# Attention kernel of four blocks: order of gate products in the second half, and the Newton steps of 1/sqrt

## The chip, the cores and the metric

One core of a Trainium2 chip runs the whole program. The metric is the device time of one execution in microseconds; the time shown is the median of three runs. TensorE (PE) multiplies matrices, VectorE (DVE) and ScalarE (ACT) work on tiles in SBUF and on PE's results in PSUM, GpSimd (POOL) does some additions and memsets, and SyncE (SP) issues most of the DMAs.

## What is computed

A sequence of 512 tokens of width 1024 goes through one block with a neighbourhood and a dilated attention between two feed-forward parts, and then through two hybrid layers. The change touches the hybrid layers and every norm. One hybrid layer, cut to what matters:

```python
h = rmsnorm(x, mix_norm)                     # x * rsqrt(mean(x*x) + eps) * gain
z = h @ w_in                                 # queries, keys, values of three attentions, latents
o_a = nsa_attention(...)                     # 8 heads: compressed keys + selected + window
o_b = swa_sink_attention(...)                # 8 heads, band of 128 keys
o_c = mla_attention(...)                     # 8 heads from two normed latents
g = sigmoid(h @ w_branch_gate)               # 512 x 3072
g_a, g_b, g_c = split(g, 3)
merged = g_a * (o_a @ w_branch_a) + g_b * (o_b @ w_branch_b) + g_c * (o_c @ w_branch_c)
x = x + merged @ w_out
```

The compressed keys and values of `nsa_attention` come from a small network, `gelu(flat @ w1) @ w2`, on overlapping blocks of 32 tokens (`compress_blocks`).

## The kernel before

Every fp32 product is split: weights and activations are each a high part and a low part (`whi`, `wlo`, `uh`, `ul`), and `gemm` (lines 143 to 145) multiplies three pairs of them for each of 8 blocks of 128 rows, so one product of 128 columns of weights with 512 tokens is 24 matmuls of 128x512. ACT makes the high part (line 88), DVE the low part (line 89).

`mix2` works on one hybrid layer. The banded attention `swa` runs 8 heads in 8 steps, then `nsa` runs 8 heads, then `mla` 8 heads. Their own matmuls are small and wait for ACT and DVE in turn: scores on PE, maximum on DVE, exponential on ACT, scaling to two fp16 parts on ACT and DVE (`halves`, lines 98 and 99), transposes on PE (line 105 in the banded attention, 995 in the others), copies on ACT, product with the values on PE (lines 1002 and 1003). Between the heads `mix2` calls `pump`, which lets generators emit other work: projections of queries and keys (`qb`, `qa`, `kva`), the compression network (`inp`, `cmp_`, `end`), the latents of `mla` (`lt`), and `gts`, the gates. One step of `gts` is one gate product: 24 matmuls, a multiplication on DVE (line 470), a tanh on ACT (line 471) and a DMA to DRAM. There are 24 such steps in a layer. Two steps share one weight load of 1 MB into `wraw`, of which there are two buffers. `gt` is the gates' tile, with two buffers. The compression network also takes its two work tiles, `hT` and `s`, from `gt`.

```python
plan = ((qb, 1, kva, 1), (inp, 1, qb, 1), (inp, 1, cmp_, 1), (qb, 1, cmp_, 1), (qa, 1, cmp_, 1), (qa, 1, cmp_, 1),
        (qa, 1, end, 1, gts, 1), (kva, 1, qa, 1, gts, 1))
for n, _ in enumerate(self.swa(QB, *kb, i, OB)):
    self.pump(*plan[n])
plan = ((lt, 2), (lt, 2, gts, 1), (lt, 1, gts, 2)) + ((gts, 3),) * 5
for h, _ in enumerate(self.nsa(QA, KS, KW, KC, VS, VC, G, OA)):
    self.pump(*plan[h])
```

So two gates stand beside `swa` (after steps 6 and 7), 18 beside `nsa`, and the last four beside the first heads of `mla` (two after each head). What is emitted is not yet the order: a scheduler of the framework (a simulated timeline) orders the instructions of each engine when the program is built, and may bring independent work forward. On the chip each engine then keeps to that order.

`rstd` (lines 165 to 188) is 1/sqrt for all norms. PE adds up squares with a column of ones (line 171), DVE forms the mean (line 173), a first guess from the bits of the number (line 175), and three steps of three instructions each on 128x2 or 128x4 numbers (lines 177 to 179). Then DVE multiplies a diagonal with the result (line 185) and PE spreads it over all partitions as a row (line 186). It is called 21 times.

Of the kernel before, what the change touches and what calls it, by code (L numbers as in the profile page):

```python
# [13 lines left out]
OP = mybir.AluOpType  # L14
# [12 lines left out]
class Core:  # L27
# [135 lines left out]
    def rstd(self, acc, n, row=True, cols=ALL, stat=None):  # L163

        nc = self.nc
        st, r = stat or self.stat(row)
        js = range(cols.start // 128, cols.stop // 128)
        s = slice(js.start, js.stop)
        ps = self.bank(self.aside)
        for j in js:  # L170
            nc.tensor.matmul(ps[:, j:j + 1], acc[:, j * 128:(j + 1) * 128], self.ones[:, 0:1], start=True, stop=True)
        a, y, t = st[:, 0, s], st[:, 1, s], st[:, 2, s]
        nc.vector.tensor_scalar(a, ps[:, s], 1.0 / n, EPS, op0=OP.mult, op1=OP.add)

        nc.vector.tensor_scalar(y.bitcast(I32), a.bitcast(I32), -0.5, 1597463007.0, op0=OP.mult, op1=OP.add)
        for _ in range(3):
            nc.vector.tensor_tensor(t, y, y, op=OP.mult)
            nc.vector.scalar_tensor_tensor(t, t, -0.5, a, op0=OP.mult, op1=OP.mult)
            nc.vector.scalar_tensor_tensor(y, t, 1.5, y, op0=OP.add, op1=OP.mult)
        if r is None:  # L180
            return st[:, 1], r
        ps = self.bank(self.aside)
        for j in js:
            d = self.dtile("dr")
            nc.vector.tensor_scalar(d, self.ident, st[:, 1, j:j + 1], None, op0=OP.mult)
            self.row_done = nc.tensor.matmul(ps[:, j * 128:(j + 1) * 128], self.ones, d, start=True, stop=True).ins
        nc.scalar.activation(r[:, cols], ps[:, cols], AF.Copy)
        return st[:, 1], r
# [5 lines left out]
    def gain(self, x, g):  # L194
# [3 lines left out]
        return h, l  # L198

    def ffn(self, uh, ul, rstd, wg, wu, wd, sink, tail=None, first=None):  # L200


# [3 lines left out]
        def up(f0, nf):  # L206
            hh, hl = [], []
            for f in range(f0, f0 + nf, 2):
# [9 lines left out]
                for i in range(2):  # L218
                    if f == 0 and tail:
                        psg = banks[i]  # L220
                    else:
                        psg = self.bank()
                        self.gemm(psg, pg[i], uh, ul)
                    if f == 0 and tail and i == 0:
                        psu = banks[2]
                    else:
                        psu = self.bank()
                        self.gemm(psu, next(pu), uh, ul)
                    g = self.t("ft")
                    nc.vector.tensor_tensor(g, psg, rstd, op=OP.mult)  # L230
                    nc.scalar.activation(g, g, AF.Silu)
                    u = self.t("ft")
                    nc.vector.tensor_tensor(u, psu, rstd, op=OP.mult)
                    nc.vector.tensor_tensor(u, u, g, op=OP.mult)
                    h, l = self.t("hh", F32R), self.t("hl", F32R)
                    self.split(h, l, u)
                    hh.append(h)
                    hl.append(l)
# [606 lines left out]
class Block2(Block1):  # L845
# [205 lines left out]
    def mix2(self, X, U, a, i):  # L1051
        nc = self.nc
# [49 lines left out]
        def queries(out, first):  # L1102
            for c0 in (first, first + 256):
                for ps in proj(c0, 256):
                    out.extend(self.stack_q(self.rope(ps, cosr, sinr), 0.125))
                    yield

        def keys_a():
            for c0 in (768, 1024):
                ka.append(self.stack_k(self.rope(next(proj(c0)), cosr, sinr)))  # L1110
                yield

        def keys_b():
            kb.append(self.stack_k(self.rope(next(proj(1816)), cosr, sinr)))
            yield
            kb.append(self.values_b(next(proj(1944)), R))
            yield

        def gates():
            nonlocal gd  # L1120
            for gd in self.gates(a["w_branch_gate_2"][i], uh, ul, R, 24, f"gates2_{i}"):
                yield

        def branches():
            yield from self.branch(gd[8:16], a["w_branch_b_2"][i], OB, ("uh", "uh"), merged, "ul")
            yield from self.branch(gd[0:8], a["w_branch_a_2"][i], OA, ("uh", "uh"), merged, "ul")


        kvb, kva, qb, qa = keys_b(), keys_a(), queries(QB, 1304), queries(QA, 0)
# [3 lines left out]
        inp, cmp_ = self.compress_in(FL, i, proj, cosr, sinr, R, flat), self.compress(a, i, flat)  # L1133
        gts, brs, lt = gates(), branches(), self.latents(a, i, proj, w_in, uh, ul, R, lat)
        KC = VC = None

        def last():
            nonlocal KC, VC
            KC, VC = next(cmp_)
            yield  # L1140
        end = last()
        plan = ((qb, 1, kva, 1), (inp, 1, qb, 1), (inp, 1, cmp_, 1), (qb, 1, cmp_, 1), (qa, 1, cmp_, 1), (qa, 1, cmp_, 1),
                (qa, 1, end, 1, gts, 1), (kva, 1, qa, 1, gts, 1))
        for n, _ in enumerate(self.swa(QB, *kb, i, OB)):
            self.pump(*plan[n])
        KS, KW = ka


        plan = ((lt, 2), (lt, 2, gts, 1), (lt, 1, gts, 2)) + ((gts, 3),) * 5
        for h, _ in enumerate(self.nsa(QA, KS, KW, KC, VS, VC, G, OA)):  # L1150
            self.pump(*plan[h])
        for h, _ in enumerate(self.mla(lat, a, i, OC)):
# [69 lines left out]
    def compress(self, a, i, flat):  # L1222

        nc = self.nc
        out = []
        for kv in range(2):
            w1 = a["a_cmp_w1_v_2" if kv else "a_cmp_w1_k_2"][i]
            hT, s = self.t("gt"), self.t("gt")
            w2 = a["a_cmp_w2_v_2" if kv else "a_cmp_w2_k_2"][i].rearrange("(k p) n -> p k n", p=128)
            w = hT[:, 128:384].rearrange("p (k n) -> p k n", k=2)  # L1230
            nc.sync.dma_start(w[:, :, 0:64], w2)
            if kv == 0:
                nc.sync.dma_start(w[:, :, 64:128], w2)

            ps = self.bank()
            for half in range(2):
                r = self.raw(8, 256)
                nc.sync.dma_start(r, w1[1024 * half:1024 * half + 1024].rearrange("(k p) n -> p k n", p=128))
                for j in range(8):
                    e = j % 2  # L1240
                    nc.tensor.matmul(ps[64 * e:64 * e + 64, 0:256], flat[kv][:, 8 * half + j].rearrange("p g n -> p (g n)"),
                                     r[:, j], start=half == 0 and j < 2, stop=half == 1 and j > 5)
            nc.scalar.activation(s[0:64, 0:256], ps[64:128, 0:256], AF.Copy)
            nc.vector.tensor_tensor(s[0:64, 0:256], ps[0:64, 0:256], s[0:64, 0:256], op=OP.add)
            yield
            ps = self.bank()
            for m in range(2):
                nc.tensor.transpose(ps[:, 64 * m:64 * m + 64], s[0:64, 128 * m:128 * m + 128], self.ident[0:64, 0:64])
            nc.scalar.activation(hT[:, 0:128], ps[:, 0:128], AF.Gelu_apprx_tanh)
            yield  # L1250
            if kv == 0:
                both = self.t("kc", F32R)
                ps = self.bank()
                for k in range(2):
                    nc.tensor.matmul(ps[:, 0:64], w[:, k], hT[:, 64 * k:64 * k + 64], start=k == 0, stop=k == 1)
                c = both[:, 0:128].rearrange("p (g e n) -> p e g n", g=2, e=2)
                self.split(c[:, 0], c[:, 1], ps[:, 0:64].rearrange("p (g n) -> p g n", g=2))
                out.append([c[:, :, g] for g in range(2)])
            else:
                c = both[:, 128:384]  # L1260
                for g in range(2):
                    ps = self.bank()
                    for k in range(2):
                        nc.tensor.matmul(ps[0:32, 0:64], hT[:, 64 * k + 32 * g:64 * k + 32 * g + 32], w[:, k, 0:64],
                                         start=k == 0, stop=k == 1)
                    o = 128 * g
                    for r in (0, 32):
                        self.split(c[r:r + 32, o:o + 64], c[r:r + 32, o + 64:o + 128], ps[0:32, 0:64], 1 / UP)
                out.append([c[0:64, 0:128], c[0:64, 128:256]])
        yield out  # L1270
# [334 lines left out]
```

## Time and profile before

| | us |
|---|---|
| median of three runs | 3258.23 (3254.02 to 3265.27) |
| the profiled execution, its own time | 3259.47 |
| its span, first to last instruction | 3257.7 |
| PE busy | 3171.5 |
| DVE busy | 1905.7 |
| ACT busy | 1480.2 |
| POOL busy | 350.7 |
| mean granted clock of PE | 0.985 |

The granted clock is a share of 2.4 GHz: 1.00 in a stretch is that level throughout, 0.50 the lower level of 1.2 GHz. Matmuls overlap in PE, so that a busy PE is not always one at its peak. Of PE's busy time and of the chain that ended last, the page gives shares; of stretches of the span, a view by windows gives the busy time of each engine and the granted clock; the view of waits says which engine stood still, for how long in all, how often, and the longest of them.

The first hybrid layer's banded attention lies from about 1265 to 1385 us, its `nsa` from there to about 1620 us; in the second layer these are 2270 to 2385 us and up to 2621 us.

### The profile page before, as it was taken

Reading aid. Unit: us, or ns where it says so; the run is one execution under the profiler, and the core shown is the slowest. Engines: PE = TensorE matmul, PEld = TensorE weight load, DVE = VectorE, ACT = ScalarE, POOL = GpSimd, SP = SyncE. Lnnn points to the kernel's source line nnn. Section 1 sums busy time; section 2 is a strip of 40 time slices with the busy share of each in tenths; the row PEclk is TensorE's granted clock in tenths of the full one; section 3 lists DMA queues with packets and bytes.
Section 4 is the critical chain, followed back from the end, with each engine's and each line's share of the span. In section 5 each row is a group of like instructions: output and inputs, shape, how many; then the busy total and the mean of one; then the engine's idle time right before and its main releaser. Section 6 shows DMA issues by size and latency. Waiting matters only on the chain.

```text
span 3257.7 us, 44744 instructions
## 1 busy us (share of the span) xinstructions
PE 3171.5 (97%) x16695; PEld 2610.2 (80%) x16695; DVE 1905.7 (58%) x3745; ACT 1480.2 (45%) x2929; POOL 350.7 (11%) x562
## 2 busy tenths in 40 slices
PE   8999899999999998999999999999999999999998
PEld 7888888778888887778777888888778878788887
DVE  5344555555744458776677544357876677544355
ACT  4323335644432335667775322234766776322233
POOL 2200231102650020000003000000000002000001
PEclk9999999999999998999999999999989999999999
DMA  5432253336132325423265323224532246332322
GB/s 147 127 104 94 88 172 114 88 118 202 57 120 91 107 70 147 137 79 102 84 188 173 113 92 104 91 91 136 156 90 95 89 141 200 126 104 91 104 84 71
DMA packets 365737, 373.39 MB, mean 115 GB/s; under 512 B 48640, under 2 KB 317824, under 8 KB 365520
## 3 DMA queue, kind: packets, MB, share of 16 engines
q1 hardware_dynamic: 358672, 358.48, 35.5%
q0 software_dynamic: 6640, 12.01, 1.4%
q8 instruction: 131, 2.15, 0.3%
q14 instruction: 86, 0.70, 0.1%
q10 hardware_dynamic: 208, 0.05, 0.0%
HBM read 320.16 MB, written 44.91 MB: 112 GB/s over the span
## 4 chain that ended last, share of the span: by engine, by line
PE 91%; DVE 4%; DMA 2%; ACT 2%; issue 1%; SPq 0%; POOL 0%; DVEq 0%; ACTq 0%; POOLq 0%
PE ps_mm L143 13%; PE ps_mm L144 13%; PE ps_mm L145 13%; PE ps_s L145 6%; PE ps_s L143 6%; PE ps_s L144 6%; PE ps_t L143 6%; PE ps_t L145 6%; PE ps_t L144 6%; PE ps_s L969 3%; PE ps_t L995 2%; PE ps_o L1002 1%; PE ps_o L1003 1%; PE ps_t L105 1%; DMA gt<-gates 1%
## 5 line engine op out<-in xcount | busy, mean ns | idle before, releaser
L88 ACT ACTIVATE whi<-wraw 128x1024 fp32r<-128x1024 f32 (+4 forms) x422 | 414.7, 990 | 823.5 <-PE ps_mm L144 259.7
L143 PE MATMUL ps_mm<-uh,whi 128*128 128x512 f32 (+2 forms) x1648 | 647.0, 393 | 5.0 <-DVE ft L1041 2.8
L145 PE MATMUL ps_mm<-uh,wlo 128*128 128x512 f32 (+2 forms) x1648 | 644.2, 391 | 0.0
L144 PE MATMUL ps_mm<-ul,whi 128*128 128x512 f32 (+2 forms) x1520 | 593.6, 391 | 3.1 <-DVE ul L92 3.1
L89 DVE TENSOR_TENSOR wlo<-wraw,whi 128x1024 fp32r<-128x1024 f32 (+4 forms) x422 | 494.6, 1177 | 161.6 <-ACT whi L88 160.0
L143 PEld LDWEIGHTS ps_mm<-uh,whi 128*128 128x128 f32 (+1 forms) x1648 | 311.7, 189 | 65.9 <-DVE ft L1041 3.2
L145 PEld LDWEIGHTS ps_mm<-uh,wlo 128*128 128x128 f32 (+1 forms) x1648 | 311.0, 189 | 60.4 <-issue 0.2
L144 PEld LDWEIGHTS ps_mm<-ul,whi 128*128 128x128 f32 (+1 forms) x1520 | 287.2, 189 | 57.8 <-DVE ul L92 3.8
L143 PE MATMUL ps_t<-uh,whi 128*128 128x512 f32 (+1 forms) x600 | 231.2, 385 | 0.0
L145 PE MATMUL ps_t<-uh,wlo 128*128 128x512 f32 (+1 forms) x600 | 230.2, 384 | 0.0
L144 PE MATMUL ps_t<-ul,whi 128*128 128x512 f32 (+1 forms) x600 | 230.1, 383 | 0.0
L145 PE MATMUL ps_s<-uh,wlo 128*128 128x512 f32 (+1 forms) x544 | 208.6, 384 | 0.0
L144 PE MATMUL ps_s<-ul,whi 128*128 128x512 f32 (+1 forms) x544 | 208.6, 383 | 0.0
L143 PE MATMUL ps_s<-uh,whi 128*128 128x512 f32 (+1 forms) x544 | 208.4, 383 | 0.0
L88 ACT ACTIVATE dh<-wraw 128x768 fp32r<-128x768 f32 (+2 forms) x102 | 89.9, 898 | 209.1 <-PE ps_mm L144 68.8
L99 DVE SCALAR_TENSOR_TENSOR ph<-p,sa,ph 128x128 f16<-128x128 f32 (+2 forms) x224 | 124.6, 565 | 30.4 <-ACT ph L98 28.4
L89 DVE TENSOR_TENSOR dl<-wraw,dh 128x768 fp32r<-128x768 f32 (+2 forms) x102 | 105.1, 1044 | 62.6 <-ACT dh L88 62.2
L969 PE MATMUL ps_s<-k,q 128*128 128x256 f32 (+1 forms) x448 | 130.7, 383 | 2.4 <-ACT p L974 2.4
L144 PEld LDWEIGHTS ps_t<-ul,whi 128*128 128x128 f32 x600 | 114.8, 191 | 21.3
L143 PEld LDWEIGHTS ps_t<-uh,whi 128*128 128x128 f32 x600 | 114.7, 191 | 21.4
L145 PEld LDWEIGHTS ps_t<-uh,wlo 128*128 128x128 f32 x600 | 114.5, 191 | 21.6
L98 ACT ACTIVATE ph<-p,sa 128x128 f16<-128x128 f32 (+2 forms) x224 | 120.4, 554 | 25.0 <-DVE sa L990 18.7
(655 smaller groups left out, 6417.4 us busy)
## 6 DMA issues: line engine op xcount, KB each, us to landing
wraw<-w_in_in SPq DMA_DIRECT2D x28, 1024.0 KB, 5.4
wraw<-w_branch_gate_in SPq DMA_DIRECT2D x24, 1024.0 KB, 5.7
wraw<-ffn_w_gate_in SPq DMA_DIRECT2D x22, 1024.0 KB, 5.5
wraw<-ffn_w_up_in SPq DMA_DIRECT2D x22, 1024.0 KB, 5.4
wraw<-w_ffn_gate_in SPq DMA_DIRECT2D x22, 1024.0 KB, 5.9
wraw<-w_ffn_up_in SPq DMA_DIRECT2D x22, 1024.0 KB, 5.4
wraw<-ffn_w_down_in SPq DMA_DIRECT2D x24, 768.0 KB, 4.4
gates<-gt SPq DMA_DIRECT2D x64, 256.0 KB, 2.1
```

The costliest lines, as they stand in the source:

```text
L88: nc.scalar.activation(hi, src, AF.Copy)
L89: nc.vector.tensor_tensor(lo, src, hi.bitcast(F32), op=OP.subtract)
L98: self.nc.scalar.activation(h, P, AF.Copy, scale=scale)
L99: self.nc.vector.scalar_tensor_tensor(l, P, scale, h, op0=OP.mult, op1=OP.subtract)
L105: self.nc.tensor.matmul(out, hl[e][:, cols], self.ident16, start=e == 0, stop=e == 1)
L143: nc.tensor.matmul(o, w[0][k], xh[k][:, cols], start=k == 0, stop=False)
L144: nc.tensor.matmul(o, w[0][k], xl[k][:, cols], start=False, stop=False)
L145: nc.tensor.matmul(o, w[1][k], xh[k][:, cols], start=False, stop=k == kc - 1)
L969: nc.tensor.matmul(ps[:, 0:n], l, r, start=i == 0, stop=i == len(mms) - 1)
L995: nc.tensor.transpose(pt[:, e, k], hl[e][:, k * 128:k * 128 + 128], self.ident16)
L1002: nc.tensor.matmul(o, v, PH[:, k], start=first and k == 0, stop=False)
L1003: nc.tensor.matmul(o, v, PL[:, k], start=False, stop=last and k == nk - 1)
```

## The change

- `rstd` replaces the three steps of three instructions by one step of three and one of four: seven small DVE instructions in place of nine, on the same tiles. Its first step is scaled by c = 0.375, which the second takes back.
- The plan beside `swa` takes six gate products in place of two: one after each of steps 2 to 7. The plan beside `nsa` takes 13 in place of 18. `mla` takes the last five in place of four; nothing is added or left out.
- The compression network's two work tiles move from `gt` to `c` and `ot`, tiles of one buffer that `nsa` uses later for its compressed probabilities and for joining heads.

```diff
-        for _ in range(3):
-            nc.vector.tensor_tensor(t, y, y, op=OP.mult)
-            nc.vector.scalar_tensor_tensor(t, t, -0.5, a, op0=OP.mult, op1=OP.mult)
-            nc.vector.scalar_tensor_tensor(y, t, 1.5, y, op0=OP.add, op1=OP.mult)
+        nc.vector.tensor_tensor(t, y, y, op=OP.mult)
+        nc.vector.scalar_tensor_tensor(t, t, -0.5 * c, a, op0=OP.mult, op1=OP.mult)
+        nc.vector.scalar_tensor_tensor(y, t, 1.5 * c, y, op0=OP.add, op1=OP.mult)
+        nc.vector.scalar_tensor_tensor(t, y, c ** -2, y, op0=OP.mult, op1=OP.mult)
+        nc.vector.tensor_tensor(t, t, a, op=OP.mult)
+        nc.vector.scalar_tensor_tensor(t, t, -10 / 3, t, op0=OP.add, op1=OP.mult)
+        nc.vector.scalar_tensor_tensor(y, t, 5.0, y, op0=OP.add, op1=OP.mult)
...
-        plan = ((qb, 1, kva, 1), (inp, 1, qb, 1), (inp, 1, cmp_, 1), (qb, 1, cmp_, 1), (qa, 1, cmp_, 1), (qa, 1, cmp_, 1),
-                (qa, 1, end, 1, gts, 1), (kva, 1, qa, 1, gts, 1))
+        plan = ((qb, 1, kva, 1), (inp, 1, qb, 1), (inp, 1, cmp_, 1, gts, 1), (qb, 1, cmp_, 1, gts, 1), (qa, 1, cmp_, 1, gts, 1),
+                (qa, 1, cmp_, 1, gts, 1), (qa, 1, end, 1, gts, 1), (kva, 1, qa, 1, gts, 1))
...
-        plan = ((lt, 2), (lt, 2, gts, 1), (lt, 1, gts, 2)) + ((gts, 3),) * 5
+        plan = ((lt, 2), (lt, 2), (lt, 1, gts, 1), (gts, 2), (gts, 3), (gts, 2), (gts, 3), (gts, 2))
...
-            hT, s = self.t("gt"), self.t("gt")
+            hT, s = self.t("c"), self.t("ot")
```

The scheduler's order moves at three places that matter here. Line numbers of the changed kernel are higher by 5 from `rstd` on.

The first is DVE beside the third and fourth steps of `swa` in the first layer (`ph` the scaled probabilities, `oc` the banded output, `rt` and `cs` the rotation of a projection, `gt` the gate). Before:

```order
L1360 TENSOR_SCALAR sa<-sa 128x4
L99 SCALAR_TENSOR_TENSOR ph<-pp,sa,ph 128x128
L99 SCALAR_TENSOR_TENSOR ph<-pp,sa,ph 128x256 x2
L931 TENSOR_TENSOR rt<-rt,cs 128x512
L932 TENSOR_TENSOR rt<-rt,cs 128x512
L933 TENSOR_TENSOR rt<-rt 128x512
L835 COPY p<-ps_t 128x256
```

And in the changed kernel:

```order
L1365 TENSOR_SCALAR sa<-sa 128x4
L99 SCALAR_TENSOR_TENSOR ph<-pp,sa,ph 128x128
L99 SCALAR_TENSOR_TENSOR ph<-pp,sa,ph 128x256
L89 TENSOR_TENSOR wlo<-wraw,whi 128x1024
L89 TENSOR_TENSOR oc<-ps_o,oc 128x512
L936 TENSOR_TENSOR rt<-rt,cs 128x512
L475 TENSOR_TENSOR gt<-ps_mm,r 128x512
L937 TENSOR_TENSOR rt<-rt,cs 128x512
L840 COPY p<-ps_t 128x256
```

The gate's split (`wlo`) and its multiplication (`gt`) now stand between the banded attention's steps.

The second is PE in the last two heads of `nsa` in the first layer (`ps_s` scores, `ps_t` transposes, `ps_o` the product with the values, `ps_mm` gates and other products). Before:

```order
L969 MATMUL ps_s<-k,q 128x512
L144 MATMUL ps_mm<-ul,whi 128x512
L145 MATMUL ps_mm<-uh,wlo 128x512
L143 MATMUL ps_mm<-uh,whi 128x512
L144 MATMUL ps_mm<-ul,whi 128x512
L145 MATMUL ps_mm<-uh,wlo 128x512
L1453 MATMUL ps_mm<-whi,x 128x512
L1454 MATMUL ps_mm<-wlo,x 128x512
```

And in the changed kernel, from the same heads:

```order
L974 MATMUL ps_s<-k,q 128x512
L976 LDWEIGHTS identb
L976 MATMUL ps_s<-mask,identb 128x128
L974 MATMUL ps_s<-k,q 128x512
L1007 MATMUL ps_o<-pp,v 128x256
L1008 MATMUL ps_o<-pp,v 128x256
L1007 MATMUL ps_o<-pp,v 128x256
L1008 MATMUL ps_o<-pp,v 128x256
L1305 MATMUL ps_o<-c,kc 128x256
L1000 LDWEIGHTS ph
L1000 MATMUL ps_t<-ident_76,ph 128x128
```

In the changed kernel 246 rows of PE follow one another there with no gate, no projection and no product of MLA's values (lines 1453 to 1455) among them: 78 transposes, 22 score matmuls and 20 each of the two value products. In the second layer it is 230 rows with 73, 20 and 20. Before the change no run without such work is over 100 rows long in the attentions of the two hybrid layers. The 19 gates that are emitted up to there have all been brought forward.

The third is DVE in the 1/sqrt after the first feed-forward part. Before:

```order
L173 TENSOR_SCALAR sm<-ps_o 128x2
L175 TENSOR_SCALAR sm<-sm 128x2
L177 TENSOR_TENSOR sm<-sm 128x2
L178 SCALAR_TENSOR_TENSOR sm<-sm 128x2
L179 SCALAR_TENSOR_TENSOR sm<-sm 128x2
...
L185 TENSOR_SCALAR dr<-ident,sm 128x128 x2
```

And in the changed kernel:

```order
L178 TENSOR_TENSOR sm<-sm 128x2
L179 SCALAR_TENSOR_TENSOR sm<-sm 128x2
L180 SCALAR_TENSOR_TENSOR sm<-sm 128x2
L181 SCALAR_TENSOR_TENSOR sm<-sm 128x2
L182 TENSOR_TENSOR sm<-sm 128x2
L183 SCALAR_TENSOR_TENSOR sm<-sm 128x2
L184 SCALAR_TENSOR_TENSOR sm<-sm 128x2
L190 TENSOR_SCALAR dr<-ident,sm 128x128 x2
```

Seven rows stand where the three rows of lines 177 to 179 stood three times; nothing comes between them.

## Rows read from the trace of the kernel before

**Rows 1.** The page: span, busy time of PE, and the chain that ended last.

```profile
span 3257.7 us, 44744 instructions
...
PE 3171.5 (97%) x16695; PEld 2610.2 (80%) x16695; DVE 1905.7 (58%) x3745; ACT 1480.2 (45%) x2929; POOL 350.7 (11%) x562
...
PE 91%; DVE 4%; DMA 2%; ACT 2%; issue 1%; SPq 0%; POOL 0%; DVEq 0%; ACTq 0%; POOLq 0%
```

**Rows 2.** Windows: us, length, busy of each engine, PEclk, DMA share, GB/s.

```profile
1265.00:1385.00 120.00, 113.37 (x715) 86.56 (x714) 93.19 (x203) 79.02 (x187) 1.20 (x8) 0.97 0.49 142
1385.00:1470.00 85.00, 80.70 (x456) 62.90 (x454) 59.86 (x174) 55.51 (x139) 3.17 (x18) 0.92 0.24 74
1470.00:1585.00 115.00, 115.00 (x708) 93.59 (x707) 78.08 (x197) 81.86 (x200) 5.87 (x34) 1.00 0.29 93
...
2270.00:2385.00 115.00, 112.58 (x713) 83.90 (x712) 89.32 (x192) 75.20 (x178) 1.20 (x8) 1.00 0.50 146
2385.00:2475.00 90.00, 85.48 (x475) 67.86 (x474) 65.50 (x188) 57.90 (x145) 3.23 (x18) 0.89 0.26 80
```

**Rows 3.** Waits of PE over the span: us in total, times, longest us.

```profile
PE ps_o L186 <- DVE dr L185: 18.8, 6, 4.8
```

**Rows 4.** Timeline of PE in a steady product: start us, us, instruction.

```profile
559.70 0.39 PE L144 MATMUL ps_mm<-ul,whi 128*128 128x512 f32 x1
...
560.38 0.39 PE L144 MATMUL ps_mm<-ul,whi 128*128 128x512 f32 x1
```

**Rows 5.** Two waits of PE before step 2 of `swa`, from its timeline.

```profile
1285.34 0.23 PE L105 MATMUL ps_t<-ident,ph 128*128 128x128 f16 x1 [1.43 <-DVE ph L99]
1286.68 0.50 PE L143 MATMUL ps_mm<-uh,whi 128*128 128x512 f32 x1 [1.11 <-ACT rt L833]
```

**Rows 6.** Groups of ACT from 1470 to 1585 us: busy us, mean ns, idle before.

```profile
L88 ACT ACTIVATE whi<-wraw 128x1024 fp32r<-128x1024 f32 x13 | 13.8, 1063 | 5.8 <-PE ps_mm L144 5.8
L471 ACT ACTIVATE gt<-gt 128x512 f32<-128x512 f32 x13 | 8.2, 632 | 0.1
L974 ACT ACTIVATION_READ_ACCUMULATOR p<-ps_s,sa 128x1 f32 x32 | 6.6, 207 | 0.0
```

**Rows 7.** Windows of two short stretches of `nsa` with little beside them.

```profile
1425.00:1434.00 9.00, 7.21 (x37) 5.46 (x36) 8.12 (x29) 7.10 (x20) 0.41 (x3) 0.73 0.53 176
...
2429.30:2438.50 9.20, 7.14 (x36) 5.40 (x35) 8.40 (x27) 7.05 (x21) 0.34 (x2) 0.68 0.51 171
```

**Rows 8.** Timeline of DVE (and of POOL beside it) in two 1/sqrt chains.

```profile
405.65 0.16 DVE L177 TENSOR_TENSOR sm<-sm 128x2 f32<-128x2 f32 x1
405.85 0.70 DVE L178 SCALAR_TENSOR_TENSOR sm<-sm 128x2 f32<-128x2 f32 x1
...
408.39 0.57 DVE L178 SCALAR_TENSOR_TENSOR sm<-sm 128x2 f32<-128x2 f32 x1
409.00 0.16 DVE L179 SCALAR_TENSOR_TENSOR sm<-sm 128x2 f32<-128x2 f32 x1
409.19 0.48 DVE L185 TENSOR_SCALAR dr<-ident,sm 128x128 f32<-128x128 f32 x2
...
405.81 3.13 POOL L156 TENSOR_TENSOR sq<-sq,ft 128x256 f32<-128x256 f32 x4 [1.59 <-ACT ft L154]
...
3249.91 0.16 DVE L177 TENSOR_TENSOR sm<-sm 128x2 f32<-128x2 f32 x1
...
3251.68 0.75 DVE L1535 TENSOR_SCALAR ft<-ps_mm,sm 128x512 f32<-128x512 f32 x1
```

More of the change, by code (lines that the diff above doesn't have):

```diff
@@ L173, in rstd @@
         nc.vector.tensor_scalar(a, ps[:, s], 1.0 / n, EPS, op0=OP.mult, op1=OP.add)
+        c = 0.375
         nc.vector.tensor_scalar(y.bitcast(I32), a.bitcast(I32), -0.5, 1597463007.0, op0=OP.mult, op1=OP.add)
-        for _ in range(3):
-            nc.vector.tensor_tensor(t, y, y, op=OP.mult)
-            nc.vector.scalar_tensor_tensor(t, t, -0.5, a, op0=OP.mult, op1=OP.mult)
-            nc.vector.scalar_tensor_tensor(y, t, 1.5, y, op0=OP.add, op1=OP.mult)
+        nc.vector.tensor_tensor(t, y, y, op=OP.mult)
[5 more added lines that the diff above has]
+        nc.vector.scalar_tensor_tensor(y, t, 5.0, y, op0=OP.add, op1=OP.mult)
         if r is None:
```

## The prediction

> **What bounds the kernel now.** I read the page first: PE is busy 97% of the span and makes up 91% of the chain that ended last [rows 1]. Little can be gained but where PE stands still or runs at its lower clock. So I went on to windows by stage [rows 2] and took two things from each: the idle time (length less PE's busy time) and the clock's loss (length times what PEclk is short of 1.00). In the first layer's banded attention that is 6.6 us of idle time and 0.03 x 120 = 3.6 us of clock, in the second layer's 2.4 us and none. The entry into `nsa` is worse: 4.3 + 6.8 and 4.5 + 9.9 us. In the middle of `nsa`, with three gates to a head, PE has no idle time at all and its clock stands at 1.00. Outside the hybrid layers the largest wait of PE is for the diagonal at the end of 1/sqrt, 18.8 us in six waits [rows 3].
>
> So the change has a place to fill (the banded attention), a place that it takes from (`nsa`, which had nothing idle), and a chain that it shortens.
>
> **The gates beside the banded attention.** One gate is 24 matmuls. Three steps take 560.38 - 559.70 = 0.68 us [rows 4], so 0.227 each, and a gate is 5.44 us of PE. Four more a layer are 21.8 us moved forward. PE's work is the same in sum; what can be gained is the idle time and the clock's loss that they cover: 10.2 + 2.4 = 12.6 us in both layers. Of the first layer's, 1.43 + 1.11 us lie before step 2, where no gate is added [rows 5], so 10.1 us are left. DVE is busy for 93 of 120 us and for 89 of 115 there [rows 2], and some waits are for its own steps, which a gate that stands between them does not shorten. I take 8 us of the 10.1. Bounds: a gate holds one of the two `wraw` buffers from one step to the next, and the second half of the compression weights and the next projection are queued behind it on SP, so it could cost some 5 us; the other bound is that PE's busy time hides waits too (a matmul in flight counts as busy), which I put at 22 us, half of the 43.5 us that the eight gates last.
>
> **The end of nsa.** The scheduler brings gates forward and then has none left: 246 and 230 rows of PE in the last two heads hold attention alone. Those of the first layer hold 78 of the 80 transposes of two heads, 22 of 32 score matmuls and 20 of 24 value products, 1.67 heads on average; I take the second layer's for the same. What does such a run cost? The middle stretch of 115 us holds four heads (32 reads of an accumulator, eight to a head) and 13 gates [rows 6]. PE less the gates is 115 - 13 x 5.44 = 44.3 us, 11.1 a head. ACT is busy 81.86 us there [rows 2]; less 13 splits and 13 tanhs, 13.8 + 8.2 us [rows 6], that is 59.9, or 15 a head. With three gates PE needs 27 us a head and ACT 20, so PE sets the pace. With none ACT needs 15 and PE 11, so ACT and the steps between the engines set it, and PE waits. For 1.67 heads: PE's own work 18.5 us, ACT's 25 us. The floor is 6.5 us a layer lost.
>
> ACT is not full in such a stretch. The nearest rows are two half heads at the entry, 9.0 and 9.2 us long with next to no product beside them, in which ACT is busy for 7.1 us, 78% [rows 7]. At that pace the run takes 25 / 0.78 = 32 us and loses 13.5. But there the latents' norm is on ACT and DVE too, DVE is busy nine tenths, and the run has none of it. So I choose 85%: 29.5 us, 11 us lost a layer, 22 in both. The upper end is a run in which PE itself is at its lower clock: 2 x 18.5 = 37 us, 18.5 lost a layer. Range of this term: 13 to 37 us.
>
> The rows of those half heads show PEclk at 0.68 and 0.73, that is, PE at 1.2 GHz for more than half of the time, after it had waited for ACT and DVE [rows 7]. The Trainium skill, page "TensorE: Matmul & The Clock Gate", section "HAM oscillation — how this bites in real kernels", says that gaps in PE's work bring the clock down to half and that the work after them starts slow. The trace agrees as far as these rows go; by that rule the run would be at the upper end, and the sum 15 us higher than mine. I hold to the 85% since ACT, not PE, has the most to do in the run.
>
> The other moves cost nothing that I can see. The latents at the entry keep nearly the same work beside them (129 and 124 matmuls of projections and gates in the two heads), so I leave the 25.5 us lost there as they are, give or take 4. The tiles `c` and `ot` are free until `nsa`, and the compression used its two `gt` buffers in the same turn as now; if that cover were gone, the first split of `nsa` would wait for the last compression matmul, which stands well ahead of it in the order.
>
> **1/sqrt.** Two of nine small DVE instructions go. Where DVE is alone they start 0.197 us apart: nine steps from 3249.91 to 3251.68 [rows 8]. Two are 0.39 us. Beside POOL nine steps last from 405.65 to 409.19, 0.393 apart, so two are 0.79 us [rows 8]. Of 21 calls, those that count are the six behind PE's waits [rows 3] and the last one before the output: three beside POOL and four alone, 3 x 0.79 + 4 x 0.39 = 3.9 us. In the other calls PE has products to do. Range: 3 to 6 us.
>
> Beside POOL every second one of these instructions takes 0.57 to 0.70 us in place of 0.16, and a POOL addition lasts 3.13 / 4 = 0.78 [rows 8]: two of DVE's get through for each of POOL's. The Trainium skill, page "SBUF — State Buffer", section "Who interferes with whom", states that a DVE instruction with two inputs in SBUF and a GpSimd instruction that reads SBUF share a port, and that the later one is fully blocked until the other is done. Taken strictly, each of the two would save a whole POOL addition, 1.57 us a chain, and the sum would be 2.4 us lower; the row shows every second one unblocked, so I take 0.79.
>
> **The sum.** Against the profiled execution's own time: 3259.5 + 22 - 8 - 3.9 = 3269.6 us. The median of the runs is 1.2 us below that execution, so 3268.4, and I say 3269.
>
> **The rivals.**
>
> 1. The starved end of `nsa` costs more than the floor and outweighs the rest: my forecast, 3269 us (3262 to 3277). For it: PE's order shows the run, and ACT needs more than PE for a head without a gate. Chance 0.44.
> 2. The run falls to the lower clock: 37 us a run, 15 us more than my sum, 3284 us. For it: 0.68 and 0.73 in the half heads. Against: the lower clock's length there is set by latents too. Chance 0.16.
> 3. The run is at ACT's floor (13 us in both layers) and the rest as in my sum: 3259.5 + 13 - 8 - 3.9 - 1.2 = 3259 us. For it: ACT's queue is never empty when scores of the next block are ready, and there are two score banks. Against: 78%. Chance 0.26.
> 4. Not slower, faster: the banded attention takes the four gates at half price, since PE's busy time there is mostly latency. Then 22 us are gained there, and with ACT's floor at the other end 3259.5 + 13 - 22 - 3.9 - 1.2 = 3245 us. It decides from the point at which the banded stretch grows by less than about 16 us for its 21.8 us of added matmuls. For it: DVE is the busier engine there and the first layer has waits for it. Against: only 12.6 us of idle time and clock are seen. Chance 0.14.
>
> **How the numbers follow.** About 0.3% (9.8 us) is what a measurement of this kernel can tell from no change, so the limits are 3248.5 and 3268.0 us. The first rival puts most of its weight above the upper limit (0.30 of 0.44), the second all of it, so slower is 0.46. The third lies within, with the first's remainder: 0.40. Faster is the fourth: 0.14. The range takes in the first three and the top of the fourth: 3249 to 3287 us, with a tenth left out at either side.
>
> **What would show it.** Right or wrong, by step. In the changed profile, the last two heads of `nsa` in each layer should show a stretch of about 30 us in which PE runs lines 974 to 1008 alone and waits for ACT (lines 979, 98, 1002 and 1003) or for DVE, with ACT over 80% busy; 25 us or less speaks for rival 3, 36 or more at a PEclk near 0.5 for rival 2. The banded stretch should be longer by 12 to 19 us with less idle time; under 12 speaks for rival 4. PE's waits for the diagonal should fall from 18.8 to about 15.5 us. I am wrong if the run is filled after all, or if the entry to `nsa` changes by more than its bound of 4 us, since it has the largest loss of all and I move nothing there.

## The result, and the profile after

The changed kernel takes 3293.75 us (median of four runs, 3284.92 to 3295.13) against 3261.28 us before: ratio 1.0097, 95% interval 1.0074 to 1.0119. It is 32 us slower. The direction was the one forecast; the time lies 7 us above the stated range of 3249 to 3287.

The profiled execution was the shortest of the four, 3284.92 us, 25.5 us above the profiled one of before. A second profile of the same kernel (the experiment e0_after) has 3295.59 us, near the median. I read both. The page of the first, its span, busy times and chain [rows 1]:

```profile
span 3283.1 us, 44668 instructions
...
PE 3182.6 (97%) x16695; PEld 2611.1 (80%) x16695; DVE 1899.1 (58%) x3703; ACT 1481.5 (45%) x2929; POOL 350.5 (11%) x562
...
PE 89%; DVE 5%; DMA 3%; ACT 2%; issue 1%; SPq 1%; POOL 0%; DVEq 0%; ACTq 0%; POOLq 0%
```

The shares of busy time do not differ from those of before. What differs is the chain: two points have gone from PE to DVE and DMA. The windows tell where. First of before, from the first exponential of the banded attention's sink to the first compressed product of `nsa` in each layer, and from the thirteenth compressed product to the last value product of `nsa` (columns as in rows 2):

```profile
1273.50:1390.00 116.50, 109.87 (x695) 83.30 (x693) 91.69 (x206) 78.06 (x185) 1.20 (x8) 0.97 0.49 145
2278.80:2400.20 121.40, 117.23 (x735) 87.12 (x734) 98.22 (x216) 84.04 (x201) 1.20 (x8) 1.00 0.50 142
...
1570.90:1619.10 48.20, 46.97 (x292) 37.25 (x292) 31.59 (x76) 34.95 (x84) 2.42 (x14) 1.00 0.30 89
2575.10:2621.00 45.90, 44.88 (x287) 36.21 (x287) 31.04 (x73) 36.10 (x86) 2.76 (x16) 1.00 0.30 90
```

Between the same instructions in the changed kernel:

```profile
1265.30:1415.40 150.10, 139.28 (x831) 106.84 (x830) 106.30 (x232) 90.66 (x209) 1.20 (x8) 0.98 0.47 140
2293.50:2433.80 140.30, 132.73 (x788) 100.73 (x786) 98.30 (x213) 83.60 (x198) 1.20 (x8) 0.96 0.47 138
...
1584.90:1619.00 34.10, 28.43 (x177) 20.89 (x177) 22.72 (x64) 26.80 (x72) 2.48 (x14) 0.85 0.09 28
2608.60:2642.60 34.00, 29.27 (x176) 21.52 (x176) 22.10 (x63) 26.05 (x71) 2.54 (x14) 0.85 0.08 23
```

Take idle time and the clock's loss of each, as the prediction did. At the end of `nsa` they were 1.2 and 1.0 us and are 10.8 and 9.8 us, of which 5.1 us each are the clock's: the starved run that was forecast is there. In the banded attention they were 10.1 and 4.2 us and are 13.8 and 13.2 us: the gates were to fill that time, and it has grown. (In the kernel with the new 1/sqrt alone, e1 below, the same two sums are 9.7 and 11.0 us, so the second stretch varies by 7 us with the plan of before.)

For the comparison of many kernels I use a finer measure, called **left** below: how much longer a stretch between two common instructions is than in the profiled execution of before, less the work of PE that moved into it (each matmul at the spacing at which its kind follows itself in dense stretches, 0.227 us for 128x512, 0.12 for 128x256, 0.05 for a transposition). The first banded stretch grew by 33.6 us and took 28.8 us of work, so 4.8 us are left.

| us left against before | ahead of the layers | banded, layers 1, 2 | entry of `nsa` | end of `nsa`, layers 1, 2 | `mla` | merging |
|---|---|---|---|---|---|---|
| changed, first profile | -7.2 | 4.8, 6.6 | -8.9 | 12.0, 11.6 | 4.6 | 3.5 |
| changed, second (e0) | -3.2 | 5.8, 5.5 | -3.4 | 13.5, 9.7 | 4.4 | 5.8 |
| 1/sqrt alone (e1) | -3.7 | -1.2, 5.1 | -2.1 | 0.1, -0.4 | 1.4 | -0.2 |
| 18 beside `nsa` (e4) | -5.8 | 5.2, 4.6 | -4.9 | -0.8, -1.4 | -0.3 | 2.6 |
| own buffer (e5) | -4.2 | -1.8, 1.2 | -6.0 | 9.0, 8.3 | 14.3 | 29.5 |
| late gates (e6) | -4.8 | -2.5, 0.2 | -11.0 | 6.8, 10.5 | 3.7 | 5.8 |
| late gates, 18 (e8) | -4.7 | -2.0, 0.0 | -0.7 | -1.9, -0.8 | 1.2 | 4.3 |
| 13 beside `nsa` alone (e9) | -3.7 | -0.1, 4.9 | -5.4 | 9.5, 6.8 | 7.7 | 6.5 |
| late gates, 16 (e12) | -4.7 | -2.1, 0.2 | -9.2 | 3.7, 4.0 | 0.6 | -0.7 |

Each row is one execution; two executions of the changed kernel differ by up to 5.5 us in a column, so only larger or repeated differences are read. The entry, `mla` and the merging are sums of both layers. The middle of `nsa` is left out, since it stays within 2 us. An experiment's number in the text that has no row here is by the same measure.

### The profile page after: what moved, and what is told of

It is laid out like the page before. It is cut to its first block, busy times and chain, and to the rows that moved or that the text cites. A ratio compares the mean times of both kernels' runs of the same rounds, so it can differ in the third digit from the quotient of the medians.

```text
span 3283.1 us, 44668 instructions
## 1 busy us (share of the span) xinstructions
PE 3182.6 (97%) x16695; PEld 2611.1 (80%) x16695; DVE 1899.1 (58%) x3703; ACT 1481.5 (45%) x2929; POOL 350.5 (11%) x562
## 4 chain that ended last, share of the span: by engine, by line
PE 89%; DVE 5%; DMA 3%; ACT 2%; issue 1%; SPq 1%; POOL 0%; DVEq 0%; ACTq 0%; POOLq 0%
PE ps_mm L143 14%; PE ps_mm L144 13%; PE ps_mm L145 13%; PE ps_t L143 6%; PE ps_s L145 6%; PE ps_s L143 6%; PE ps_s L144 6%; PE ps_t L145 6%; PE ps_t L144 6%; PE ps_s L974 2%; PE ps_t L1000 2%; PE ps_o L1007 1%; PE ps_o L1008 1%; PE ps_t L105 1%; DMA gt<-gates 1%
## 5 line engine op out<-in xcount | busy, mean ns | idle before, releaser
L143 PE MATMUL ps_mm<-uh,whi 128*128 128x512 f32 (+2 forms) x1648 | 648.2, 394 | 14.4 <-ACT whi L88 5.9
L979 ACT ACTIVATE p<-ps_s,sa 128x128 f32<-128x128 f32 (+1 forms) x192 | 101.1, 528 | 74.0 <-DVE sa L978 55.0
L144 PEld LDWEIGHTS ps_t<-ul,whi 128*128 128x128 f32 x600 | 114.5, 191 | 21.5
```

What stands on the lines that cost most here:

```text
L143: nc.tensor.matmul(o, w[0][k], xh[k][:, cols], start=k == 0, stop=False)
L144: nc.tensor.matmul(o, w[0][k], xl[k][:, cols], start=False, stop=False)
L979: nc.scalar.activation(P[:, 0:w], ps[:, 0:w], AF.Exp, bias=st[:, 0:1], accum_out=st[:, 1:2])
```

## The experiments

Ratios are to runs of the kernel before on the same chip, five rounds each, with the 95% interval. In the expectations "theory A" is what I held at that point.

**The parts by themselves, and the whole again.** e1_rstd keeps the new 1/sqrt and takes both plans and the tiles back:

> Only the new 1/sqrt; plans and tiles as before. Theory A, read from the two traces (the changed kernel is 7.2 us ahead when the first banded attention begins and gains 2 us more at the last norm): 9 us faster, ratio 0.997, and each of PE's waits for the diagonal shorter. Rival B, the prediction's own term: 3.9 us, ratio 0.9988, since the two removed instructions are all that goes; the other 5 us would then be the scheduler's new order and would not come back here.

Measured: 3255.97 us, 0.9986 (0.9977 to 0.9995), so 4.6 us faster. The prediction's 3.9 us hold; the 9 us that I had read from one pair of traces do not.

e2_sched is the opposite, the whole change with the three old steps of 1/sqrt:

> Only the plans and the tiles; 1/sqrt as before. Theory A: the layers lose 34 us of the profiled times (two runs without gates at 11 to 12.6 us, the banded attentions and the entries 2 us net, mla and what follows it 8 to 9 us), so 34 us and the 9 us of 1/sqrt on top of the whole change's time less 9: ratio 1.011 to 1.014. Rival B, the prediction's terms: 22 - 8 = 14 us slower, ratio 1.004.

Measured: 3287.73 us, 1.0084 (1.0070 to 1.0097), 27 us slower. It lies between the two theories. The plans are the loss.

e3_tiles takes only this line of the change:

```diff
-            hT, s = self.t("gt"), self.t("gt")
+            hT, s = self.t("c"), self.t("ot")
```

> Only the compression network's two work tiles, from gt to c and ot; plans and 1/sqrt as before. Theory A: nothing, ratio 1.000 within 0.002, since c and ot are free until nsa. Rival C: single buffers hold the compression or the first heads of nsa up, 3 to 8 us slower, ratio 1.001 to 1.0025, and part of what the banded attention lost in the whole change is this.

Measured: 3259.69 us, 1.0001 (0.9992 to 1.0010). The tiles cost nothing, as the prediction had it.

> The whole change once more, for a second profile. Its first profile came from its fastest execution, 3284.9 us, against 3293.5 to 3295.1 in the three others. Theory A: ratio 1.009 to 1.011, and a profile near 3294 us shows the missing 9 us as PE at its lower clock in stretches where it waits, not as work. Rival: the 9 us lie in other waits, spread over the span.

Measured: 3292.53 us, 1.0097 (1.0082 to 1.0111). The two profiles of one kernel differ by 10.7 us, and the mean granted clock is 0.986 in the shorter and 0.980 in the longer. About half of the difference is the entry to `nsa` in the second layer; the same stretch, first of the shorter and then of the longer execution:

```profile
2418.00:2508.00 90.00, 86.84 (x501) 68.94 (x500) 66.07 (x172) 58.19 (x141) 3.33 (x18) 0.96 0.30 88
```

```profile
2423.00:2518.00 95.00, 92.21 (x501) 73.32 (x499) 65.83 (x172) 58.14 (x140) 3.38 (x18) 0.89 0.29 83
```

The same 501 matmuls take 5 us more at 0.89 than at 0.96, with about 3 us idle in both. So in this stretch it is the clock, where PE waits often, and not other waits; the other half of the difference is not followed.

**The end of nsa.** e4_nsa18 is the whole change with one line taken back, so that `nsa` has its 18 gates and `mla` none:

```diff
-        plan = ((lt, 2), (lt, 2), (lt, 1, gts, 1), (gts, 2), (gts, 3), (gts, 2), (gts, 3), (gts, 2))
+        plan = ((lt, 2), (lt, 2, gts, 1), (lt, 1, gts, 2)) + ((gts, 3),) * 5
```

> The whole change, but nsa keeps the 18 gates that it had, so that six stand beside the banded attention and none beside mla. In PE's order no run without gates is over 90 matmuls long now (142 to 163 in the changed kernel). Theory A (the runs at the end of nsa, 11 to 12.6 us each, are the largest part of the +32 us): about 23 us faster than the whole change, less what mla loses without its five gates, 3 to 5 us a layer: 3274 us, ratio 1.003 to 1.006. Rival B: the shortage only moves to mla, whose first two heads have no branch product beside them yet, and the time stays at 3288 us or more, ratio 1.008 or more.

Measured: 3257.70 us, 0.9997 (0.9989 to 1.0006): the loss against the kernel before is gone, more than theory A expected, and nothing moved to `mla`. The windows from the thirteenth compressed product to the last value product of `nsa`, in each layer:

```profile
1588.60:1635.60 47.00, 46.20 (x293) 37.35 (x293) 30.74 (x74) 35.66 (x86) 2.76 (x16) 1.00 0.44 136
2591.40:2641.60 50.20, 50.20 (x311) 40.50 (x311) 33.79 (x79) 37.16 (x90) 2.42 (x14) 1.00 0.48 140
```

PE has hardly an idle moment, at the full clock.

e9_nsa13_alone is the converse. It takes the new 1/sqrt and the tiles, but two gates beside the banded attention, as before (that part of its edit is not shown); `nsa` has 13, and `mla` the other nine:

```diff
-            self.pump(gts, 2)
+            self.pump(gts, 5)
```

> Only the shortage: two gates beside the banded attention as before, 13 beside nsa, and the other nine beside the first two heads of mla (five and four). The new 1/sqrt and the tiles c and ot are in. PE's order has the runs of 144 and 154 matmuls without a gate at the end of nsa, and the banded attention is as before. Theory A: 16 us lost at the end of nsa in the traces and up to 12 us in mla, less 4.6 us of 1/sqrt: 3272 to 3284 us, ratio 1.0035 to 1.007. Rival: without six gates beside the banded attention the run costs the whole 32 us: ratio 1.008 or more; or, if the banded attention was the cause, nothing: 0.9985 to 1.0005.

Measured: 3279.48 us, 1.0050 (1.0034 to 1.0066). Against the new 1/sqrt alone that is 0.0064, or 20.9 us (give or take 6) for taking five gates from `nsa`. The expectation puts some of it into `mla`; there I had cut `nsa` at its last compressed product, which left the last part of its last head to `mla`. Cut at the last value product, as in the table, 16.3 us are at the end of `nsa`:

```profile
1557.10:1592.00 34.90, 29.02 (x193) 20.36 (x192) 24.94 (x71) 28.86 (x77) 2.42 (x14) 1.00 0.17 55
2576.60:2610.50 33.90, 28.58 (x203) 21.19 (x203) 25.32 (x70) 29.41 (x80) 2.48 (x15) 1.00 0.22 71
```

PE is idle for 5.9 and 5.3 us, ACT is busy for 83% and 87% of the time. The rest of the 20.9 us is not at the end of `nsa`: `mla` and the merging have 6.3 and 6.7 us more left than in e1.

**The gates beside the banded attention.** In the changed kernel's chain there stands a load of gate weights, in both layers; in the chain of before none does there. The chain in the first layer (start us, us, what):

```profile
1328.08 1.90 PE ps_mm L1246 x16
1329.98 0.35 SPq L1236
...
1330.44 5.87 DMA wraw<-w_branch_gate_in
...
1336.33 1.06 ACT whi L88
...
1337.44 0.50 PE ps_mm L143
...
1339.20 0.43 PE ps_mm L143
```

SP's timeline shows why it starts so late:

```profile
1300.45 0.37 SPq L1243 DMA_DIRECT2D wraw<-a_cmp_w_v_in  x1
...
1315.45 0.38 SPq L1243 DMA_DIRECT2D wraw<-a_cmp_w_v_in  x1
...
1330.44 0.44 SPq L133 DMA_DIRECT2D wraw<-w_branch_gate_in  x1
```

The two buffers of `wraw` are given to the compression's weights, one at 1300 and the other at 1315 us, and all 32 matmuls that read them (line 1246) run between 1328.0 and 1332.4 us. The first sixteen, which free the first buffer, end at 1329.98 us, and the gate's load starts at 1330.44. (SP itself issues four loads of `rt` and one of `c` from 1326.27 to 1330.33 us, ahead of the gate's load in its order. So the buffer and SP's order let the load go within 0.4 us of each other, and no run takes them apart.) PE waits for the weights, and for ACT's split of them:

```profile
1337.44 0.50 PE L143 MATMUL ps_mm<-uh,whi 128*128 128x512 f32 x1 [3.87 <-ACT whi L88]
```

After this wait matmuls follow at 0.43 us in place of 0.23 (the chain's last line): from 1338.6 to 1341.5 us the granted clock is 0.50, the level of 1.2 GHz. Three experiments bear on this.

e5_own_buffer gives the gates a weight buffer of their own, half as large, so that each load is for one gate in place of two; to make room, `gt` gets one buffer in place of two:

```diff
-        for c in range(0, n, 2):
-            for e, p in enumerate(self.wgen(w, c * 128, 256)):
+        for c in range(0, n, 1 if "wg" in self.tags else 2):
+            for e, p in enumerate(self.wgen(w, c * 128, 128 if "wg" in self.tags else 256, tag="wg")):
...
-        with self.phase(f"mix2_{i}", cs=(4, 512), ...
-                        gt=(2, 512), p=(2, 512), ...
+        with self.phase(f"mix2_{i}", wg=(1, 1024), cs=(4, 512), ...
+                        gt=(1, 512), p=(2, 512), ...
```

> The whole change, but the gates' weights have a buffer of their own (512 KB, one gate at a time) in place of a turn in the two of wraw, and gt has one buffer in place of two. Theory A (six gates gain nothing beside the banded attention because the weights of the third wait for a buffer that the compression's weights hold, so that PE stands 3.9 us in the first layer and 1.1 us in the second at ACT's split and runs on at the lower clock): these waits are gone, 5 to 10 us faster than the whole change, ratio 1.007 to 1.008. Rival B: the banded attention is set by DVE's and ACT's own chain, which the gates' splits and products lengthen: time as the whole change's, 1.009 to 1.011.

Measured: 3305.46 us, 1.0138 (1.0124 to 1.0151). As a time it speaks against theory A, but the trace shows two things. The banded stretches lose 12 us less than in the changed kernel, and the wait is gone. The merging loses 29.5 us, where finished gates are loaded back through `gt`, which is now single. PE waits 12.8 us there for the products with `gt` (line 508 of that kernel), a wait that the changed kernel's trace does not have; that the single `gt` is the cause was not tried by itself. The banded stretches:

```profile
1267.90:1411.20 143.30, 136.33 (x831) 104.58 (x829) 106.09 (x233) 91.24 (x209) 1.20 (x8) 1.00 0.49 139
2303.00:2444.40 141.40, 136.65 (x828) 103.09 (x826) 104.67 (x228) 89.29 (x207) 1.20 (x8) 1.00 0.49 142
```

The first holds the same 831 matmuls as in the changed kernel in 6.8 us less, at the full clock.

e6_gates_late leaves buffers alone and asks for no gate while the compression holds them:

```diff
-        plan = (..., (inp, 1, cmp_, 1, gts, 1), (qb, 1, cmp_, 1, gts, 1), (qa, 1, cmp_, 1, gts, 1),
-                (qa, 1, cmp_, 1, gts, 1), (qa, 1, end, 1, gts, 1), (kva, 1, qa, 1, gts, 1))
+        plan = (..., (inp, 1, cmp_, 1), (qb, 1, cmp_, 1), (qa, 1, cmp_, 1, gts, 1),
+                (qa, 1, cmp_, 1, gts, 1), (qa, 1, end, 1, gts, 2), (kva, 1, qa, 1, gts, 2))
```

> The whole change, but the six gates beside the banded attention stand later: one after steps 4 and 5, two after steps 6 and 7, none after 2 and 3. Theory A: the gate that waited behind the compression's weights is no longer asked for then, 3 to 8 us faster than the whole change, ratio 1.0075 to 1.009. Rival B (DVE's and ACT's chain): no change, since the same work lies beside the same eight steps, ratio 1.009 to 1.011.

Measured: 3269.13 us, 1.0025 (1.0014 to 1.0035), 23.5 us less than the whole change where 3 to 8 were expected. The banded stretches give 14 of it (first profile: 11.4 us left, now -2.3), and the end of `nsa` 6 (23.6, now 17.3).

e7_gates_first keeps a gate in each of the six steps, but emits it ahead of the step's other work (`(gts, 1, inp, 1, cmp_, 1)` and so on), so that its load stands ahead of the compression's:

> The whole change, but each of the six gates beside the banded attention is emitted at the head of its step, ahead of the projection and of the compression's weights, so that its own weights take the buffer first. Theory A: as with a buffer of its own, 3 to 8 us faster than the whole change, ratio 1.0075 to 1.009. Rival C: the wait for a buffer moves to the compression's weights and with them to the first heads of nsa, which need its keys: time as the whole change's, 1.009 to 1.011.

Measured: 3271.96 us, 1.0043 (1.0031 to 1.0056); the banded stretches have -4.2 and -1.0 us left. The compression, whose loads now stand behind the gates', makes the entry to `nsa` 2 us longer than in e1 by the same measure (0.0 left), which is within the spread of that column. So two different orders of the same gates and the buffer of their own each take the loss away; what they share is that a gate's load does not stand behind the compression's. A longer chain of DVE and ACT beside the banded attention, the rival in e5 and e6, would have stayed in all three, since the same six gates lie beside it.

**Both cures.** e8_18_late joins the late gates with 18 beside `nsa`:

> Both cures together: nsa keeps its 18 gates, and the six beside the banded attention stand late (one after steps 4 and 5, two after 6 and 7). Theory A (two separate causes: a shortage of gates from the end of nsa on, some 32 us in the traces, and a gate's weights behind the compression's beside the banded attention, some 12 us): no run without gates, banded attention 6 to 7 us shorter in each layer than with the six as changed, so 3245 to 3250 us, ratio 0.9955 to 0.998. Rival B: what the late gates gave came from the end of nsa too, and nothing is left to gain: 3258 us, ratio 0.999 to 1.000.

Measured: 3251.61 us, 0.9969 (0.9958 to 0.9980). e11_18_first joins gates-first with 18:

> As the late gates with 18 beside nsa, but with the six gates emitted at the head of their steps, so that their weights take the buffer ahead of the compression's. Theory A: as with late gates, 3245 to 3252 us, ratio 0.9955 to 0.9985. Rival B: 3258 us, ratio 0.999 to 1.000.

Measured: 3253.15 us, 0.9976 (0.9966 to 0.9987). Both are faster than either kernel; 4.6 of the 10.1 and 7.8 us are the new 1/sqrt's.

**How many gates nsa needs.** e10_mla_3 asks what the fifth gate beside `mla` costs (`self.pump(gts, 3)` in place of 2):

> The whole change, but mla takes its five gates as three and two beside its first two heads, in place of two, two and one: the fifth no longer stands beside the first branch products, whose loads of finished gates share the tile gt with it. The runs at the end of nsa stay (163 and 142 matmuls). Theory A: what mla loses against before (6.8 and 5.2 us in the first trace) comes from that meeting, 6 to 12 us faster than the whole change, ratio 1.006 to 1.008. Rival B: mla loses because PE starts it late and with nothing brought forward, whatever the place of the fifth gate: no change, ratio 1.009 to 1.011.

Measured: 3288.24 us, 1.0077 (1.0063 to 1.0091). The ratio is theory A's, the trace is not: `mla` has 2.7 us left in place of 4.5, and the 6.5 us gained are no more than the uncertainty of the difference (6.6). This stays open.

> Late gates beside the banded attention (six), 16 beside nsa, two beside the first head of mla. Between the late gates with 18 (ratio 0.9969) and with 13 (1.0025). The last head of nsa still has 27 to 29 of the gates' matmuls; no long run without gates is left. Theory A (what costs is the run at the end of nsa and what mla loses behind it): no loss, ratio 0.996 to 0.998. Rival B (every gate that stands beside mla costs there, run or none: 18 us for five): two fifths of it, 7 us, ratio 0.9985 to 1.000, with mla 2 us a layer longer than its added work.

Measured: 3250.85 us, 0.9973 (0.9961 to 0.9984): with late gates, 16 do as well as 18. The trace has 7.7 us left at the end of `nsa`, paid for by an entry and a merging that lose less (the plan with 16 puts no gate into the second head and one in place of two into the third). `mla` has 0.6 us left, not the 4 of rival B.

> Late gates beside the banded attention (six), 14 beside nsa, four beside mla's first two heads. PE's order has runs of 96 matmuls (first layer) and 129 (second) without a gate at the end of nsa, against 141 and 155 with 13. Theory A: loss by the length of the run, 225 of 296 matmuls of the 18 us, 14 us: ratio 1.0005 to 1.002. Rival B: four fifths of 18 us, the same 14 us; the trace tells them apart, by how much of it lies in mla and how much at the end of nsa.

Measured: 3256.84 us, 0.9988 (0.9979 to 0.9997), better than either theory. At the end of `nsa` 6.1 and 8.3 us are left, in `mla` 1.4: the loss stands where theory A puts it. So with late gates this column holds -2.7, 7.7, 14.4 and 17.3 us for 18, 16, 14 and 13 gates, some 4 us for each gate that is taken from the plan, which is 2 us in each layer.

> Four late gates beside the banded attention (two after steps 6 and 7 each), 18 beside nsa, two beside mla. Theory A: no run without gates, and less to hide beside the banded attention: between the two late ones (0.9986 with two gates, 0.9969 with six), ratio 0.997 to 0.9985. Rival: four fit without a wait where six did not, ratio below 0.9965.

Measured: 3259.05 us, 0.9994 (0.9985 to 1.0003). Neither. Four late gates gained nothing over the two of e1 (0.9986), and did worse than six by 8.2 us. The trace has some 5 us left at the end of the first layer's `nsa`, where six late gates leave none: its last 36 matmuls take 7.6 us, at a granted clock of 0.75. Why they stand alone there, though 18 gates are emitted, was not pursued.

## Why the prediction was wrong in size

Forecast were 10.1 us of loss (22 - 8 - 3.9), measured are 31.6. Of the 21.5 us between them 11.6 are the gates beside the banded attention, the step that failed; 11.7 appear only when the parts stand together; the other two terms are off by about 1 us each, to the other side.

**1/sqrt: right.** 3.9 us forecast, 4.6 measured alone (1.6 to 7.5). PE's waits for the diagonal fell from 18.8 us [rows 3] to 15.4, where 15.5 was forecast:

```profile
PE ps_o L191 <- DVE dr L190: 15.4, 5, 4.0
```

Beside POOL the steps last from 403.70 to 406.44 us, 2.74 us, against 3.54 before [rows 8], so 0.80 us a chain are saved where 0.79 was taken:

```profile
403.70 0.16 DVE L178 TENSOR_TENSOR sm<-sm 128x2 f32<-128x2 f32 x1
...
406.44 0.83 DVE L190 TENSOR_SCALAR dr<-ident,sm 128x128 f32<-128x128 f32 x2
```

The strict reading of the rule on the shared port (the Trainium skill, page "SBUF — State Buffer", section "Who interferes with whom"), 1.57 us a chain, did not come about.

**The end of nsa: right in place and mechanism, near in size partly by luck.** Forecast were 29.5 us of a run at 85% of ACT, and 22 us lost in both layers. In the changed kernel PE runs the attention alone from 1584.9 to 1615.4 us in the first layer (163 matmuls) and for 28.3 us in the second (153), and ACT is busy for 84% and 86% of these 30.5 and 28.3 us. The run of the second layer, and below it the one of the first layer in e9, which holds nearly the same matmuls:

```profile
2610.50:2638.80 28.30, 23.57 (x155) 16.77 (x153) 19.61 (x57) 24.43 (x67) 2.54 (x14) 0.88 0.05 12
```

```profile
1561.80:1589.40 27.60, 21.78 (x155) 14.72 (x153) 19.95 (x57) 24.27 (x66) 2.42 (x14) 1.00 0.09 24
```

At a granted clock of 0.88 in one and 1.00 in the other the runs differ by 0.7 us: ACT and the steps between the engines set the length, as forecast, and PE's clock adds little (the run of 163 in the first layer took 30.5 us at 0.88 and 32.1 at 0.79 in the two executions of the changed kernel). Left at the end of `nsa` are 23.6 and 23.2 us in the two profiles of the changed kernel, but 16.3 with 13 gates alone. The 20.9 us that e9 measures as a time are near the 22 partly by luck, since `mla` and the merging, which the prediction put at nothing, are in them. Of the rivals, ACT's floor (13 us) is too little. The rival of the lower clock named the nearest total, 3284 us, but not by its mechanism: over the whole end of `nsa` the clock stands at 0.85 in both layers, not near 0.5, and where it stood at 1.00 (e9) the run still cost 16 us. By the rule of the Trainium skill that was weighed there (page "TensorE: Matmul & The Clock Gate", section "HAM oscillation — how this bites in real kernels"), that gaps bring the clock down to half and the work after them starts slow, the prediction put such a run at the lower level throughout; the granted clocks, 0.76 to 1.00 in the six such stretches of the two profiles and e9, lie between.

**The gates beside the banded attention: the step that failed.** Forecast was a gain of 8 us. Alone (e4 against e1; the four gates come from `mla` there) they cost 0.0011, 3.6 us, give or take 4; in the traces of the changed kernel the banded stretches lose 11 us against before, 7.5 against e1, which has 3.9 left with two gates. The step took the idle time that it saw for time that gates could fill. That time can be filled: placed late, the six gates gain 5.5 us (e8 against e1, give or take 4.6), and moving them from where the change put them to there gives 9.1 us. What it missed is when a gate's weights can arrive. It did name the buffer, but the wrong way round: as a gate that holds a buffer from the projection and the compression behind it. It is the compression that holds the buffers: the one that the gate takes from 1300.45 to 1329.98 us, 29.5 us, and the other with it from 1315.45 on. A bound of +5 us stood in the text, which is where the 3.6 us lie, but the value chosen was at the other side.

**What the sum left out.** `mla` and the merging behind it were costed at nothing and have 8 to 10 us left in the traces of the changed kernel; with no gates in `mla` (e4, e8) it is 2 to 6. No run isolates what they wait for. Against that, the entry has 3.4 us less left in one profile and 8.9 in the other, within and beyond the bound of 4, and much of this is the clock of the one execution.

**The parts do not quite add up.** Alone they make -4.6 + 20.9 + 3.6 = 19.9 us; together 31.6 are measured. The four ratios leave some 8 us of uncertainty in the difference of 11.7. With late gates and with gates first the parts do add (10.8 against 8.2 us, and 13.1 against 14.0). The traces put 7 us of the rest at the end of `nsa`: 23 us are left there in the changed kernel, 16.3 with 13 gates alone. The order of PE agrees: the scheduler's longest run of matmuls without a gate is 163 and 153 there, and 154 and 144 with 13 gates alone, and these runs last 30.5 and 28.3 us against 27.6 and 23.6. The same holds for e2, which with the old 1/sqrt is 4 us faster than the whole change (give or take 6.5) where the parts say 4.6 slower: its second layer's run has 144 matmuls and lasts 23.6 us, and 16 us are left. So part of the loss hangs on how the scheduler happens to order the same plan. Where the other 5 us are, if they are real, stays open.

**The range.** The median lies 8.8 us above the changed kernel's first profiled execution, while before's lay 1.2 us below its own. A range that is built on one profile needs a term for the difference between executions of one order, 10.7 us between the two profiles here, half of it shown to be the clock's.

## What to carry to other kernels

Independent work that is moved into a stage must have its data there in time: before counting the idle time as filled, follow its load back to the buffer that it takes, and ask who holds that buffer and until when. Work that covers a latency-bound stage is spent when it is moved: divide the stage into what each engine needs per head without the cover, since the next engine in line (here ACT, busy for 84 to 88% of these runs) gives the length of the run. Where a scheduler brings such work forward, it is the last heads that run dry here, whatever the plan says of them.

## What the runs showed of the hardware

In these traces the granted clock differs between executions of the same order, in stretches where PE waits: at the entry of the second layer's `nsa` 0.96 in one and 0.89 in the other, 5 us for 90. At the end of `nsa` in the first layer it was 0.85 and 0.76 in the two executions of the changed kernel, and 1.00 in the kernel that had the same kind of run with 13 gates alone, though PE was idle for a sixth of it. In the middle of `nsa`, where PE has no idle time, it was 1.00 in each of them. What the clock costs depends on what sets the length: 5 us of 90 at the entry, between 0.96 and 0.89, but 0.7 us of 28 in a run that ACT paces, between 1.00 in one kernel and 0.88 in another with nearly the same matmuls.
